# LayerNorm sums taken from additions that are made anyway, a deferred second pass, and two weight slabs from another DMA queue

## The chip, the cores and the metric

The kernel runs on one Trainium2 chip, on all 8 cores (two dies of four), each core with one row of the batch (2048 tokens of 1024). The metric is the device time of the slowest core in microseconds. Some executions fall into a slow state, in which one die is granted a lower clock (0.82 to 0.98 instead of 0.996) and takes up to 18% longer; all comparisons below are between fast executions.

## The reference, cut to what matters

```python
x = layer_norm(ALPHA * x + mix, ln1_w, ln1_b)          # mix: gated convolution and retention, projected
ff = square(relu(x @ w_ff1)) @ w_ff2
ple = sigmoid(x @ w_ple_gate) * (p @ w_ple_proj)
x = layer_norm(ALPHA * x + ff + ple, ln2_w, ln2_b)

def layer_norm(x, w, b):
    mu = mean(x); var = mean(square(x - mu))
    return (x - mu) * rsqrt(var + 1e-5) * w + b
```

A core thus has two LayerNorms over 16 blocks of 128 tokens. The first runs beside retention (blocks 0 to 7) and beside the first feed-forward matmuls (blocks 8 to 15). The second runs in two halves, of which the last ends the kernel. In that last half the second feed-forward matmul is done in seven products (M1 to M7) that VectorE adds into the float32 accumulator `xacc`.

## The kernel before

Helpers record every operation, so all matmuls are "L195" in the profile (transposes on TensorE L199), all `tensor_tensor` L202, all `scalar_tensor_tensor` L213, all activations L226, all DMAs L239. An operation waits for exactly the resources that it names. `bg` is a queue of generators; every `bg.step()` records the next piece of one of them, so the places of `yield` set where LayerNorm stands among the other VectorE work.

```python
# first LayerNorm, blocks 0 to 7 (fine: blocks 0 to 3)
for hf in range(2):
    bn_stats(half hf)                                  # VectorE
    if fine: yield
bn_aggr; rstd = var + eps                              # VectorE
if fine: yield
rstd = pow(rstd, -0.5)                                 # GpSimd
yield
buf = (buf - mean) * w                                 # VectorE, first pass
yield
buf = buf * rstd + b                                   # VectorE, second pass
yield

# statistics of the other blocks: two ScalarE passes over the block, each with an accumulator
def row_stats(b, v, r):
    for k, (fn, sc) in enumerate(((AF.Copy, 1.0 / D), (AF.Square, D ** -0.5))):
        h.act(junk[:], v, fn, [r], ["junk", ("mva", b)], scale=float(sc), accum=lna[:, b, 4 + k:5 + k])

# loads of first-matrix slabs
h.dma("pool", ring[i][:], src, ("ring", i), rd, r)     # all on GpSimd's queue

# last phase, after product (m, p): additions, statistics, and two units later the normalizing
ff2_adds(s_, m, p)
if m == "M4": row_stats(4 + p, ...); due.append((i + 2, 4 + p))
if m == "M5" and p < 3: act_stats(p, 1)
if m == "M7": act_stats(p, 0); due.append((i + 2 - (p == 2), p))
...
# the end: block 3, in two products of 256 columns
ff2_add(3, 0, BANK[1]["M5"] + 3, -1); last_stats(2, 512, 1024)
for q in range(2):
    ...16 matmuls of 256 columns...; xacc -= product; last_stats(q, ...)        # bn_stats
```

Of the kernel before, what the change touches and what calls it, by code (L numbers as in the profile page):

```python
# [17 lines left out]
D = 1024  # L18
# [171 lines left out]
class H:  # L190
# [21 lines left out]
    def stt(self, out, in0, scalar, in1, op0, op1, reads, writes):  # L212
        self.P.op("dve", lambda e: e.scalar_tensor_tensor(out=out, in0=in0, scalar=scalar, in1=in1,  # L213
                                                          op0=op0, op1=op1), reads, writes)
# [91 lines left out]
def build_nc():  # L306
# [59 lines left out]
    lnst = at("lnst", [128, 8, 20], F32, o, [("lnst", i) for i in range(8)]); o += 640  # L366
    lna = at("lna", [128, 8, 8], F32, o, [("lna", i) for i in range(8)]); o += 256
# [77 lines left out]
    xs4 = at("xs4", [128, 4, 512], BF16, o_x1b)  # L445
    hT = at("hT", [128, 32, 1024], BF16, o_sin, [("hT", f, a) for f in range(32) for a in range(2)])
# [5 lines left out]
    with ExitStack() as st:  # L452
# [70 lines left out]
        def load_slab(nm, g, i):  # L523
            r = rname[i]
            if nm in SUMS:
                n = SUMS.index(nm)
                h.dma("sp", ring[i][:], s_w2[n, g], ("ringh", i), [("s_w2", n, g)], r)
                return
            if nm in PRODS[1]:
                nm, g = "ff2", g + {"M2": 0, "M5": 6}[nm]  # L530
            src, rd = wsrc[nm][g], []
            if nm in ("ff1", "gate"):
                k = g + 8 * (nm == "gate")
                src, rd = s_wb[k], [("s_wb", k)]
            h.dma("pool", ring[i][:], src, ("ring", i), rd, r)
# [241 lines left out]
        def gen_ln(buf, rbuf, w_t, b_t, rw, rb, slot, fine=False):  # L777
            st6 = lnst[:, slot, 0:12]
            mv = lnst[:, slot, 12:14]
            rstd = lnst[:, slot, 14:15]  # L780
            rl, rr = ("lnst", slot), ("rstd", slot)
            for hf in range(2):
                P.op("dve", lambda e, hf=hf: e.bn_stats(out=st6[:, hf * 6:(hf + 1) * 6],
                                                        in_=buf[:, hf * 512:(hf + 1) * 512]),
                     [rbuf], [rl])
                if fine:
                    yield
            P.op("dve", lambda e: e.bn_aggr(out=mv, in_=st6), [rl], [rl])
            h.ts("dve", rstd, mv[:, 1:2], LN_EPS, ALU.add, [rl], [rr])
            if fine:  # L790
                yield
            h.tt("pool", rstd, rstd, neghalf[:, 0:1], ALU.pow, [rr, "neghalf"], [rr])
            yield
            h.stt(buf, buf, mv[:, 0:1], w_t[:], ALU.subtract, ALU.mult, [rbuf, rl, rw], [rbuf])
            yield
            h.stt(buf, buf, rstd, b_t[:], ALU.mult, ALU.add, [rbuf, rr, rb], [rbuf])
            yield

        def act_stats(b, hf):

            v = xacc[:, b, hf * 512:(hf + 1) * 512]
            for k, (fn, sc) in enumerate(((AF.Copy, 1.0 / D), (AF.Square, D ** -0.5))):
                h.act(junk[:, 0:512], v, fn, [("xa", b)], ["junk", ("lna", b)], scale=float(sc),
                      accum=lna[:, b, 2 * hf + k:2 * hf + k + 1])

        def row_stats(b, v, r):

            for k, (fn, sc) in enumerate(((AF.Copy, 1.0 / D), (AF.Square, D ** -0.5))):
                h.act(junk[:], v, fn, [r], ["junk", ("mva", b)], scale=float(sc),
                      accum=lna[:, b, 4 + k:5 + k])  # L810

        def act_norm(b, halves=False):

            mv, rstd = lna[:, b, 4:6], lna[:, b, 6:7]
            if halves:
                h.tt("dve", mv, lna[:, b, 0:2], lna[:, b, 2:4], ALU.add, [("lna", b)],
                     [("mva", b)])
            h.stt(rstd, mv[:, 0:1], mv[:, 0:1], mv[:, 1:2], ALU.mult, ALU.subtract,
                  [("mva", b)], [("rsa", b)])
            h.ts("dve", rstd, rstd, -1.0, ALU.mult, [("rsa", b)], [("rsa", b)], s2=LN_EPS,  # L820
                 op1=ALU.add)
            h.tt("pool", rstd, rstd, neghalf[:, 0:1], ALU.pow, [("rsa", b), "neghalf"], [("rsa", b)])

        def norm_pass(k, b, v, r, w_t, rw):


            if k == 0:
                h.stt(v, v, lna[:, b, 4:5], w_t, ALU.subtract, ALU.mult, [r, ("mva", b), rw], [r])
            else:
                h.stt(v, v, lna[:, b, 6:7], w_t, ALU.mult, ALU.add, [r, ("rsa", b), rw], [r])  # L830
# [15 lines left out]
        def mix_part(b, hf, slab, rs, bank):  # L846
# [5 lines left out]
            if b < 8:  # L852
# [3 lines left out]
                  [xr, RP[bank]], [x1r(b)])  # L856
# [3 lines left out]
        def gen_ln1(b):  # L860
            yield from gen_ln(x1v(b), x1r(b), lnt[0], lnt[1], "ln1w", "ln1b", b % 8, b < 4)
# [17 lines left out]
        def gen_norm1(b):  # L879


            act_norm(b - 8)
            yield
            for k in range(2):
                norm_pass(k, b - 8, x1v(b), x1r(b), lnt[k][:], ("ln1w", "ln1b")[k])
                yield
# [99 lines left out]
        for b in range(8, 16):  # L986
# [9 lines left out]
            if 9 <= b < 15:  # L996
                row_stats(b - 9, x1v(b - 1), x1r(b - 1))
# [210 lines left out]
        def phase_ff1_first():  # L1208
# [13 lines left out]
            for n, (g, a) in enumerate(order):  # L1222
# [8 lines left out]
                for f in range(4):  # L1231
# [6 lines left out]
                    if n < 2 and f == 1:  # L1238
                        row_stats(6 + n, x1v(14 + n), x1r(14 + n))
# [165 lines left out]
        def ff2_add(b, hf, bank, sign):  # L1405
            v = xacc[:, b, hf * 512:(hf + 1) * 512]
            h.tt("dve", v, v, ps[bank][:], ALU.add if sign > 0 else ALU.subtract,
                 [RP[bank], ("xa", b)], [("xa", b)])
# [14 lines left out]
        def ff2_adds(s_, m, p):  # L1423
            for (a, hf), sign in PRODS[s_][m][1]:
                ff2_add(4 * a + p, hf, BANK[s_][m] + p, sign)
# [4 lines left out]
        def phase_ff2_first():  # L1430
# [47 lines left out]
            for m in PRODS[s_]:  # L1478
                for i, (j, p) in enumerate(PJ if m in ("M4", "M7") else JP):
# [3 lines left out]
                    if j == 1:  # L1483
                        ff2_adds(s_, m, p)
                        if m in ("M4", "M7"):
                            b = p + 4 * (m == "M4")
                            row_stats(b, xacc[:, b, :], ("xa", b))
# [5 lines left out]
        def phase_ff2_last():  # L1493
# [8 lines left out]
            due = []  # L1502
            for i, (m, p, j) in enumerate(order):
                while due and due[0][0] <= i:
                    bg.add(gen_last(due.pop(0)[1]))
# [8 lines left out]
                if (m, p) == ("M7", 2):  # L1514
                    if j == 0:
                        ff2_add(2, 0, BANK[1]["M5"] + 2, -1)
                    ff2_product(s_, m, j, p, *slabs[m, j], bank=6)
                    if j == 1:
                        ff2_add(2, 0, 6, -1)
                else:  # L1520
                    ff2_product(s_, m, j, p, *slabs[m, j])
                if j == 1:
                    if (m, p) != ("M7", 2):
                        ff2_adds(s_, m, p)
                    if m == "M2":
                        prefetch(30 + 2 * (p == 3))
                    if m == "M4":
                        row_stats(4 + p, xacc[:, 4 + p, :], ("xa", 4 + p))
                        due.append((i + 2, 4 + p))
                    if m == "M5" and p < 3:  # L1530
                        act_stats(p, 1)
                    if m == "M7":
                        act_stats(p, 0)
                        due.append((i + 2 - (p == 2), p))
                bg.step(2 + ((m, p, j) == ("M5", 3, 0)))

            ff2_add(3, 0, BANK[1]["M5"] + 3, -1)
            last_stats(2, 512, 1024)
            for q in range(2):
                qs = slice(q * 256, (q + 1) * 256)  # L1540
                for c in range(16):
                    lt, rl = left(s_, "M7", c, 3)
                    slab, rs = slabs["M7", c // 8]
                    h.mm(ps[7 - 2 * q][:, 0:256], lt, slab[:, c % 8, qs], c == 0, c == 15, rl + rs,
                         [RP[7 - 2 * q]])
                v = xacc[:, 3, qs]
                h.tt("dve", v, v, ps[7 - 2 * q][:, 0:256], ALU.subtract, [RP[7 - 2 * q], ("xa", 3)],
                     [("xa", 3)])
                last_stats(q, q * 256, (q + 1) * 256)
                if q == 0:  # L1550
                    bg.step()
# [6 lines left out]
        st18 = lnst[:, 6:8, :].rearrange("p a b -> p (a b)")[:, 0:18]  # L1558

        def last_stats(k, c0, c1):  # L1560

            P.op("dve", lambda e: e.bn_stats(out=st18[:, k * 6:(k + 1) * 6], in_=xacc[:, 3, c0:c1]),
                 [("xa", 3)], [("lnst", 6), ("lnst", 7)])

        def gen_last(b):

            mv, rstd = lna[:, b, 4:6], lna[:, b, 6:7]
            buf, rb = xacc[:, b, :], ("xa", b)
            if b != 3:
                act_norm(b, b < 4)  # L1570
            else:
                P.op("dve", lambda e: e.bn_aggr(out=mv, in_=st18), [("lnst", 6), ("lnst", 7)],
                     [("mva", b)])
                h.ts("dve", rstd, mv[:, 1:2], LN_EPS, ALU.add, [("mva", b)], [("rsa", b)])
                h.tt("pool", rstd, rstd, neghalf[:, 0:1], ALU.pow, [("rsa", b), "neghalf"],
                     [("rsa", b)])
            yield
            n = 2 if b in (2, 3) else 1
            w_ = D // n
            parts = [(buf[:, k * w_:(k + 1) * w_], slice(k * w_, (k + 1) * w_), (rb, "part", k))  # L1580
                     for k in range(n)]
            for v, cols, r in parts:
                h.stt(v, v, mv[:, 0:1], lnt[2][:, cols], ALU.subtract, ALU.mult,
                      [rb, ("mva", b), "ln2w"], [r])
            yield
            row = (8 + b) * 128
            for k, (v, cols, r) in enumerate(parts):
# [102 lines left out]
```

## Time and profile before

| what | before |
|---|---|
| time, median of 4 runs | 786.84 us (786.61 to 787.08) |
| span of the slowest core in the profile | 785.1 us (core 4) |
| TensorE busy | 749.4 us |
| TensorE waits for the first loads | 13.8 us |
| TensorE waits in the middle | about 10 us |
| from the last matmul's end to the end | 11.67 us |

TensorE is the bound, so only places where it stands still can give time back. The timeline of the kernel before, core 4, near 225 us (start, duration, engine, line, operation, output<-input; in brackets the idle time before, and who ended it):

```profile
224.91 1.27 POOL L202 TENSOR_TENSOR qr<-ra,ra 128x512 bf16<-128x512 f32 x1 [3.05 <-DVE ra L202]
225.29 1.98 DVE L213 SCALAR_TENSOR_TENSOR xacc<-xacc,lnst,ln1b 128x1024 f32<-128x1024 f32 x1
```

The second normalizing pass stands beside GpSimd's rotary sum and takes 1.98 us, where the first pass, alone, takes 1.27. The same view at the end:

```profile
769.76 3.66 PE L195 MATMUL ps<-ring,ring 128*128 128x256 bf16 x32
...
770.76 0.16 DVE L202 TENSOR_TENSOR lna<-lna 128x2 f32<-128x2 f32 x1 [1.73 <-ACT junk L226]
...
777.64 0.42 DVE L202 TENSOR_TENSOR xacc<-xacc,ps 128x256 f32<-128x256 f32 x1 [0.17 <-DVE lnst L1562]
```

VectorE waits 1.73 us for ScalarE's statistics of block 2, and adds the last product at 777.64, while the last matmul ended at 769.76 + 3.66 = 773.42. Call this 4.22 us the *lateness* of the last addition, and the 7.45 us from there to the end of the span the *last chain*. The two sum to the tail of 11.67 us.

### The profile page before, as it was taken

The numbers are of one execution on the slowest core, as the hardware profiler recorded it, in microseconds if no ns is written. First come the engines' busy times: TensorE is split into PE (matmuls) and PEld (weight loads), VectorE is DVE, ScalarE is ACT, GpSimd is POOL, SyncE is SP. The second block draws the span as 40 slices with busy tenths as digits, with TensorE's granted clock in tenths as the row PEclk, the third lists the DMA queues.
The fourth block names the chain that finished last, engine by engine and source line by source line (L and its number), as shares of the span: only waits on it lengthen the run. The fifth ranks groups of instructions, "written<-read, shape, count | busy, mean of one in ns | idle before, by whom it ended". The sixth has DMA issues, their size and how long they took to land.

```text
span 785.1 us, 12424 instructions; the slowest of 8 cores (780.9 to 785.1 us)
## 1 busy us (share of the span) xinstructions
PE 749.4 (95%) x3880; PEld 354.2 (45%) x3880; DVE 538.3 (69%) x743; ACT 343.1 (44%) x688; POOL 211.6 (27%) x242
## 2 busy tenths in 40 slices
PE   3999999999999999998999999999999999999994
PEld 1444445555555445443444444454444444444442
DVE  4565964557975596977756987744666769766666
ACT  2222216554556379585672200067777662100341
POOL 9100025755356401132450000000354450000111
PEclk9999999999999999999999999999999999999997
DMA  9998188981889860788539878477369676376232
GB/s 121 165 172 196 28 110 109 144 150 54 115 122 117 225 202 34 302 262 287 162 134 157 173 233 187 143 221 229 108 208 298 219 240 215 114 180 134 85 141 98
DMA packets 30384, 129.45 MB, mean 165 GB/s; under 512 B 3744, under 2 KB 5920, under 8 KB 23584
## 3 DMA queue, kind: packets, MB, share of 16 engines
q0 software_dynamic: 10160, 50.86, 38.9%
q1 hardware_dynamic: 19296, 76.23, 28.4%
q10 hardware_dynamic: 864, 1.57, 0.6%
q8 instruction: 32, 0.52, 0.3%
q14 instruction: 32, 0.26, 0.1%
HBM read 131.27 MB, written 45.61 MB: 225 GB/s over the span
## 4 chain that ended last, share of the span: by engine, by line
PE 83%; DVE 6%; issue 3%; DMA 3%; POOL 2%; ACT 2%; DVEq 0%; ACTq 0%; POOLq 0%
PE ps L195 81%; DMA xT<-xT 3%; PE ps L199 2%; DVE xacc L202 1%; DVE ring L202 1%; DVE xacc L213 1%; ACT junk L226 1%; POOL lna L202 1%; ACT tR L226 1%; DVE ycat L202 1%; POOL wc L239 1%; DVE ps L202 1%; DVE eb L202 1%; POOL xT L239 1%; DVE ra L202 0%
## 5 line engine op out<-in xcount | busy, mean ns | idle before, releaser
L195 PE MATMUL ps<-ring,ycat 128*128 128x512 bf16 x1088 | 244.0, 379 | 0.3 <-DVE ra L202 0.2
L195 PE MATMUL ps<-ycat,ring 128*128 128x512 bf16 x832 | 184.9, 379 | 4.3 <-DVE ring L202 1.8
L195 PEld LDWEIGHTS ps<-ring,ycat 128*128 128x128 bf16 x1088 | 105.6, 98 | 125.5 <-issue 1.7
L195 PEld LDWEIGHTS ps<-ycat,ring 128*128 128x128 bf16 x832 | 80.7, 98 | 103.1 <-issue 7.5
L195 PE MATMUL ps<-xT,wc 128*128 128x512 bf16 x384 | 86.1, 386 | 13.8 <-DMA wc<-wc 12.9
L202 POOL TENSOR_TENSOR hT<-tR 128x512 bf16<-128x512 f32 x48 | 57.9, 1210 | 149.4 <-ACT tR L226 149.3
L226 ACT ACTIVATE tR<-ps 128x512 f32<-128x512 f32 x128 | 72.7, 595 | 37.6 <-PE ps L195 35.6
L202 DVE TENSOR_TENSOR xacc<-xacc,ps 128x512 f32<-128x512 f32 (+1 forms) x83 | 54.3, 677 | 49.7 <-PE ps L195 47.9
L226 ACT ACTIVATE junk<-xacc 128x1024 fp8e5<-128x1024 f32 (+1 forms) x36 | 32.9, 914 | 84.6 <-DVE xacc L202 78.5
L195 PEld LDWEIGHTS ps<-xT,wc 128*128 128x128 bf16 x384 | 37.4, 99 | 62.0 <-issue 20.2
L195 PE MATMUL ps<-ring,hT 128*128 128x512 bf16 x256 | 56.9, 379 | 0.0
L226 ACT ACTIVATE yn<-ps,colT 128x128 f32<-128x128 bf16 x64 | 29.3, 458 | 47.0 <-PE ps L199 42.5
L202 POOL TENSOR_TENSOR lna<-lna,neghalf 128x1 f32<-128x1 f32 x24 | 25.6, 1066 | 87.5 <-DVE lna L209 80.7
L226 ACT ACTIVATE hT<-tR 128x512 bf16<-128x512 f32 x72 | 45.4, 630 | 4.9
L226 ACT ACTIVATE ycat<-ps 128x1024 bf16<-128x1024 bf16 x16 | 16.2, 1012 | 69.5 <-PE ps L199 69.5
L202 DVE TENSOR_TENSOR ycat<-hT 128x2048 bf16<-128x2048 bf16 x36 | 44.2, 1244 | 1.6
L239 POOL DMA_DIRECT2D ring<-w_ff x12 | 6.5, 546 | 138.7 <-PE ps L195 104.9
L202 DVE TENSOR_TENSOR ring<-ring,ring 128x2048 bf16<-128x2048 bf16 x32 | 38.9, 1221 | 6.0 <-DMA s_w<-ring 2.5
L226 ACT ACTIVATE sg<-ps 128x512 f32<-128x512 f32 x32 | 19.0, 597 | 48.3 <-DVE tR L202 23.3
L202 DVE TENSOR_TENSOR ps<-ps,eb 128x512 f32<-128x512 f32 x48 | 33.6, 700 | 7.8 <-DVE eb L202 3.7
L195 PEld LDWEIGHTS ps<-ring,hT 128*128 128x128 bf16 x256 | 24.9, 98 | 29.3
L202 DVE TENSOR_TENSOR eb<-eb,ps 128x512 f32<-128x512 f32 x24 | 16.4, 685 | 27.3 <-ACT tR L226 27.0
(117 smaller groups left out, 1008.1 us busy)
## 6 DMA issues: line engine op xcount, KB each, us to landing
ring<-s_wb POOLq DMA_DIRECT2D x12, 1024.0 KB, 10.7
ring<-w_ff POOLq DMA_DIRECT2D x12, 1024.0 KB, 11.4
s_w<-ring SPq DMA_DIRECT2D x20, 512.0 KB, 3.5
s_w<-ring SPq DMA_DIRECT2D x10, 1024.0 KB, 5.6
ring<-s_w SPq DMA_DIRECT2D x20, 512.0 KB, 6.6
ring<-s_w SPq DMA_DIRECT2D x10, 1024.0 KB, 7.3
s_wb<-w_ff POOLq DMA_DIRECT2D x8, 1024.0 KB, 15.3
out<-xacc SPq DMA_DIRECT2D x14, 512.0 KB, 3.7
```

The lines of the kernel that those rows point to most:

```text
L195: self.P.op("pe", lambda e: e.matmul(out, lhsT=lhsT, rhs=rhs, start=start, stop=stop, skip_group_check=skip), reads, writes)
L199: self.P.op("pe", lambda e: e.transpose(out=out, in_=in_, identity=ident), reads, writes)
L202: self.P.op(eng, lambda e: e.tensor_tensor(out=out, in0=in0, in1=in1, op=op), reads, writes)
L213: self.P.op("dve", lambda e: e.scalar_tensor_tensor(out=out, in0=in0, scalar=scalar, in1=in1, op0=op0, op1=op1), reads, writes)
L226: self.P.op("act", lambda e: e.activation(out=out, in_=in_, func=func, **kw), reads, writes)
L239: self.P.dma(eng, lambda e: e.dma_start(out=out, in_=in_, **kw), key, reads, writes)
```

## The change

The intent: get the sum of each row from the addition that writes the row (an accumulator output), so that bn_stats goes from VectorE and one of two passes from ScalarE; let the first pass of a block run while ScalarE still squares, and defer the second behind the next product's additions; load two slabs earlier. The core of the diff, cut:

```diff
-            for hf in range(2):
-                P.op("dve", ... e.bn_stats(...))              # and bn_aggr, + eps, pow
+        def squares(n, i, v, r, out=junk, ro="junk"):
+            h.act(out[:, 0:v.shape[-1]], v, AF.Square, [r], [ro, ("sq", n)],
+                  scale=float(D ** -0.5), accum=lns[:, n, i:i + 1])
+        def mean(n):                                          # (sum0 + sum1) / D, VectorE
+        def root(n, halves=False):                            # m*m - squares, VectorE
+            ...
+            h.ts("pool", var, var, LN_EPS, ALU.add, [r], [r])
+            h.tt("pool", var, var, neghalf[:, 0:1], ALU.pow, [r, "neghalf"], [r])
...
             h.stt(x1v(b)[:, cols], xs, ALPHA, ps[bank][:], ALU.mult, ALU.add,
-                  [xr, RP[bank]], [x1r(b)])
+                  [xr, RP[bank]], [x1r(b), ("sm", b)], accum_out=lns[:, b, hf:hf + 1])
...
         def gen_ln1(b):
-            yield from gen_ln(...)
+            squares(...); yield
+            mean(b); root(b); yield
+            for k in range(2):
+                norm_pass(k, ...); yield
...
+            if nm == "ff1" and g in (2, 6):
+                h.dma("act", ring[i][:], src, ("ringa", i), rd, r)
+                return
             h.dma("pool", ring[i][:], src, ("ring", i), rd, r)
...
+            def finish():
+                while second:
+                    next(second.pop(0))                       # the second pass and its store
...
                         ff2_adds(s_, m, p)
                     if m == "M2":
                         prefetch(30 + 2 * (p == 3))
+                    finish()
                     if m == "M4":
-                        row_stats(4 + p, ...); due.append((i + 2, 4 + p))
+                        squares(4 + p, ...)
+                        second.append(gen_last(4 + p))
+                        next(second[0])                       # first pass and root, now
```

The matmuls and their order are the same in both kernels.

## The prediction

> **What bounds the kernel now.** I read the page's busy shares first, then who makes TensorE wait, then busy time by stretch, then the timeline around each place where TensorE stands still. All lines are of the kernel before, core 4, the slowest: span 785.1 us against a median time of 786.84 us, so I carry differences of the span over to the time. The page's first row:
>
> ```profile
> PE 749.4 (95%) x3880; PEld 354.2 (45%) x3880; DVE 538.3 (69%) x743; ACT 343.1 (44%) x688; POOL 211.6 (27%) x242
> ```
>
> TensorE is busy 749.4 us, and 785.1 - 749.4 = 35.7 us is all that a change which leaves the matmuls alone can win. The order of instructions on TensorE and on SyncE is the same in both programs. The waits view (engine, line, waited for: us, times, longest):
>
> ```profile
> PE ps L195 <- DMA wc<-wc: 12.9, 3, 10.9
> PE ps L195 <- DVE ring L202: 2.1, 2, 1.8
> PE ps L195 <- DVE ps L202: 2.1, 4, 0.8
> PE ps L195 <- ACT tR L226: 1.5, 2, 0.8
> PE ps L199 <- POOL kr L202: 1.1, 1, 1.1
> PE ps L199 <- DVE ob L202: 1.1, 1, 1.1
> PE ps L199 <- DVE xacc L202: 0.9, 1, 0.9
> PE ps L195 <- DMA xT<-xT: 0.9, 2, 0.7
> ```
>
> The first and last rows, 13.8 us, are the loads at the start, which the change does not touch. The busy-by-stretch view shows no matmul after 774 us: from the last matmul's end at 773.4 to 785.1 is a tail of 11.7 us. That leaves about 10.2 us in the middle: 2.5 at 200 to 270 us (retention with the first LayerNorm), 3.7 at 340 to 380, 1.0 at 496 to 513, 1.4 at 540 to 556, 0.7 at 636 to 642, 0.2 near 756, the rest crumbs. Two places need their timelines. The first (start, duration, engine; in brackets the idle time before and who ended it):
>
> ```profile
> 338.69 1.11 POOL L239 DMA_DIRECT2D ring<-s_wb  x2
> ...
> 350.74 1.23 DVE L202 TENSOR_TENSOR ring<-ring 128x2048 bf16<-128x2048 bf16 x1 [4.34 <-DMA ring<-s_wb]
> ...
> 354.54 1.22 DVE L202 TENSOR_TENSOR ring<-ring,ring 128x2048 bf16<-128x2048 bf16 x1
> ...
> 355.90 7.93 PE L195 MATMUL ps<-ycat,ring 128*128 128x512 bf16 x36 [1.80 <-DVE ring L202]
> ```
>
> VectorE waits 4.34 us for two weight slabs whose loads GpSimd issued at 338.69, and TensorE then waits 1.80 us for the weight sum. In the full timeline GpSimd issues them only after a store of x1 (336.19) and a power (337.33) ahead of them in its queue. The second place is the tail:
>
> ```profile
> 774.07 1.47 DVE L202 TENSOR_TENSOR xacc<-xacc,ps 128x512 f32<-128x512 f32 x2
> ...
> 775.65 0.69 DVE L1562 BATCH_NORM_STATS2 lnst<-xacc 128x6 f32<-128x512 f32 x1
> 776.51 0.42 DVE L202 TENSOR_TENSOR xacc<-xacc,ps 128x256 f32<-128x256 f32 x1 [0.17 <-DVE lnst L1562]
> ...
> 778.69 0.24 DVE L1572 BATCH_NORM_AGGREGATE lna<-lnst 128x2 f32<-128x18 f32 x1
> ...
> 779.34 0.92 POOL L202 TENSOR_TENSOR lna<-lna,neghalf 128x1 f32<-128x1 f32 x1 [6.77 <-DVE lna L206]
> 780.79 1.41 DVE L213 SCALAR_TENSOR_TENSOR xacc<-xacc,lna,ln2b 128x512 f32<-128x512 f32 x2 [0.28 <-DVE xacc L213]
> ```
>
> Block 3's last three additions start at 774.07, with nearly no gap behind: VectorE is in arrears. The M5 product they need ended at 769.9, but VectorE was still normalizing block 2, for which it had waited 1.73 us on ScalarE's two statistics passes.
>
> **What the Trainium skill says.** "VectorE: DVE Perf Modes", section "Two Vector instructions with no wait between them": an operation that also writes out its accumulator is two instructions, the main one and an accumulator read. No VectorE operation before has one; ScalarE's form shows as 0.18 to 0.22 us of read after each pass. My estimate for VectorE's is 0.1 us. "SBUF — State Buffer", section "Who interferes with whom": a VectorE instruction with two SBUF inputs shuts out a GpSimd instruction that reads SBUF until it is done. The trace agrees: the [128,1] power takes 0.54 us alone and 1.45 beside a 1.28 us normalizing pass. "ScalarE: Activation LUTs", section "What ACT_TABLE_LOAD costs": 186 ns plus 0.833 ns an element with immediate scale; that gives 1.04 us for 1024 and 0.61 for 512, where the trace has 1.06 and 0.63; for the new width of 256 I take 0.40.
>
> **The change part by part.**
> (1) Sums come free with additions that are made anyway: accumulator outputs on the output projection's 32 evictions and on the last addition into each half row. Cost: about 65 reads of 0.1 us, 6 us of VectorE time, nearly all beside matmuls.
> (2) For blocks 0 to 7 of the first LayerNorm, two bn_stats (0.69 each), the aggregate (0.21) and the 0.15 epsilon add go from VectorE; a mean (0.15) and a variance (0.21) come. Saving 1.4 us a block, 11 us in all, against a square pass on ScalarE of 1.06 + 0.18 us each. For 23 of the other 24 row blocks ScalarE loses its Copy pass, the same 1.24 us each (1.6 for the split ones). So both engines are lighter, while GpSimd gets one more small operation a block.
> (3) In retention, 200 to 230 us, the order of VectorE changes: the first normalizing pass (1.28) now stands ahead of the `ob` and `vb` evictions, behind the wait for ScalarE's squares, and the second comes before the rotary products instead of after the masked scores. In before, that second pass ran beside GpSimd's rotary sum and took up to 2.04 us. Going through one 12.5 us round with the row durations, VectorE has 9.5 us of work instead of 11.5. The 1.1 us wait for `kr` goes, but the masked scores come some 1 us later and may cost 0.2 to 0.3 in a round. Net -0.5 us.
> (4) Slabs 2 and 6 are loaded from ScalarE's queue, right after the fourth feed-forward group. That group's matmuls end near 326 (16 groups of 1.73 us and four sets of transposes from 296), 12 us ahead of 338.69; at the same 12 us of transfer the data land near 339, before VectorE wants them at 346.4. The 4.34 us wait goes and so does TensorE's 1.80. The next two slabs, 3 and 7, are still on GpSimd, issued at 355.78 after a store that follows VectorE; they can go at about 352.5, when their slots are free. Of the 0.82 us wait at 373.8, behind a 2.28 us wait for these slabs, about 0.55 goes. Together -2.35 us.
> (5) At 496 to 513 and at 540 to 556 TensorE waits for a VectorE backlog of additions and 1.23 us sums; accumulator reads in it cost +0.1 each: +0.2 us.
> (6) The tail. The first pass of block n now runs while ScalarE squares, and the second is postponed behind the next product's additions, so VectorE waits for nothing. Going by the matmuls' ends: block 2's first pass ends by 768.8, its variance by 769.3, block 3's M5 addition (product done at 769.7) by 770.5, block 2's second pass by 771.9, the two additions ready by then at 773.0. So VectorE is free when the last product ends at 773.2 (0.2 earlier: the wait near 756 goes as well). Then: addition and read to 773.85; 256 squares 0.40 + 0.19 on ScalarE to 774.6; square sum and mean to 775.0; first half pass to 775.7; variance, two small operations 0.33 apart, to 776.1; second half pass to 776.7, GpSimd shut out till then; epsilon and power to 777.7; two half passes to 779.2. Before, that end was at 782.2. Gain 3.0 us, with the 2.9 us of the last output's DMA the same.
>
> Sum: -0.5 - 2.35 + 0.2 - 3.0 = -5.65 us: 786.84 becomes 781.2 us.
>
> **The rivals.**
> A: the accumulator read costs more than 0.1 us, say 0.25, or holds the next instruction. For it: ScalarE's own read is 0.19. Against: VectorE's [128,1] operations take 0.15 and start every 0.33 even when dependent. It would hit the LayerNorm rounds and the tail (M2 and M4 leave VectorE only some 1 us spare in 6.9): 1 to 2 us back, 782.5 to 783.
> B: a new wait in retention. ScalarE's square pass stands in order before the `qkT` copy, and VectorE waits for it with `ob` behind. ScalarE is free from 204.8 to 207.9 in the round I read, and the squares need 206.6 to 207.9: it fits with no margin. If each of four rounds loses 0.5 us, the time is 783.5.
> C: the early load is hidden or collides: slabs 2 and 6 travel with the weight-sum stores, and TensorE finds its next wait at the sums of 357 to 364, which stand in the same order. Against: the DMA share at 270 to 340 is 0.53, and the engines have room. It would give 783.5, with only the tail won.
> D: waits in the middle all vanish, because VectorE has 11 us less to do: then up to 4 us more, 777. Against: `ob` at 266 and the chains at 364 and 553 are latencies through three engines.
>
> **Range and chances.** Steps (4) and (6) rest on timelines that I could follow one by one, and each could miss by 1.5 us; (3) by 1.0. With the rivals this makes 778.6 to 784.2 us. A gain over 2% needs 771.1, so 15.7 us out of the 21.9 that lie outside the start's loads, where the tail cannot vanish: chance 0.01. A loss of 2% would need a new bound, and no engine but TensorE is over 70%: 0.01.
>
> **What would show each step right or wrong.** (1): a read row of about 0.1 us after each accumulating addition. (3): no wait for `kr` near 228, and waits on `PT` or `qkT` below 0.3 us. (4): the slab loads in ScalarE's queue near 327, no idle VectorE before the sum near 346, no 1.80 us wait. (6): the last addition within 0.2 us of the last matmul's end, and some 8.9 us from that end to the span's end instead of 11.7. I am wrong if the slabs land late, if VectorE is still in arrears at the last product, or if TensorE's waits between 190 and 270 us grow.

## The result, and the profile after

The changed kernel takes 781.22 us (median of 9 runs, 781.02 to 781.37), the kernel before 786.52 us (median of its eight fast runs in the same rounds; over all its 13 runs, one of them slow, 786.76). The ratio is 0.9931 with a 95% interval of 0.9921 to 0.9940. A ratio here is the mean time of one kernel's fast runs over that of the other's of the same rounds, so it is not quite the ratio of the medians quoted. The prediction was 781.2 us. The spans of the cores went from 780.9-785.1 to 776.9-779.2 us. The page's first row, and who makes TensorE wait, for the changed kernel, core 7, its slowest (engine, line, waited for: us, times, longest):

```profile
PE 748.7 (96%) x3880; PEld 354.4 (45%) x3880; DVE 527.8 (68%) x792; ACT 327.3 (42%) x658; POOL 219.7 (28%) x272
```

```profile
PE ps L195 <- DMA wc<-wc: 13.5, 4, 10.2
PE ps L195 <- ACT tR L226: 1.7, 2, 0.9
PE ps L195 <- DVE ps L202: 1.3, 3, 0.6
PE ps L199 <- DVE ob L202: 1.0, 1, 1.0
PE ps L199 <- DVE xacc L213: 1.0, 1, 1.0
...
PE ps L195 <- ACT sg L226: 0.4, 1, 0.4
...
PE ps L195 <- DVE PT L202: 0.2, 1, 0.2
```

VectorE and ScalarE are lighter (538.3 to 527.8, 343.1 to 327.3 us), but that alone is worth nothing. What counts is that the waits for `kr` (1.1) and for the weight sum (1.8; a second one of 0.4 stays, in the lines left out) are gone. One wait is new on every whole core: 0.4 us for the gate `sg`. Another, for `tR` just before it, comes on some cores only (0.3 us on core 7, 0.7 on core 4): there VectorE waits for a late slab of the second matrix at 424 us (3.23 and 3.54 us; on core 1 not at all) and is in arrears afterwards. In the kernel before, core 4 waits 2.13 us for it, and TensorE not. The slab loads, same core:

```profile
328.50 1.28 ACTq L239 DMA_DIRECT2D ring<-s_wb  x2
...
344.91 1.23 DVE L202 TENSOR_TENSOR ring<-ring 128x2048 bf16<-128x2048 bf16 x1
...
350.30 0.54 POOL L239 DMA_DIRECT2D ring<-s_wb  x1
```

ScalarE issues slabs 2 and 6 ten microseconds earlier than GpSimd did, and the sum at 344.91 has no bracket: nobody waited. GpSimd issues slab 3 at 350.30 and slab 7 at 351.74, where core 4 before issued both at 355.78. The end, same core:

```profile
766.31 3.66 PE L195 MATMUL ps<-ring,ring 128*128 128x256 bf16 x32
766.59 0.69 DVE L213 SCALAR_TENSOR_TENSOR xacc<-ps,xacc 128x512 f32<-128x512 f32 x1
767.21 0.08 DVE L213 DVE_READ_ACCUMULATOR xacc<-ps,xacc 128x1 f32 x1
767.66 1.41 DVE L213 SCALAR_TENSOR_TENSOR xacc<-yb,lns,ln2b 128x512 f32<-128x512 f32 x2 [0.38 <-POOL lns L202]
769.00 0.68 DVE L213 SCALAR_TENSOR_TENSOR xacc<-ps,xacc 128x512 f32<-128x512 f32 x1
...
770.73 0.42 DVE L213 SCALAR_TENSOR_TENSOR xacc<-ps,xacc 128x256 f32<-128x256 f32 x1 [0.17 <-DVE lns L202]
...
771.87 0.16 DVE L202 TENSOR_TENSOR lns<-lns 128x1 f32<-128x1 f32 x1 [0.70 <-ACT junk L226]
```

The last matmul ends at 766.31 + 3.66 = 769.97, and its addition starts at 770.73: lateness 0.76 us instead of 4.22. The last chain is 8.47 us instead of 7.45, the tail 9.23 instead of 11.67.

Where the time came from, read from the windows view as TensorE's idle time in each stretch. Two cores of each profile lack some matmul records and show 0.3 to 0.7 us more idle in several stretches, so I use whole cores:

| stretch, us | what runs | before, core 4 | after, core 4 |
|---|---|---|---|
| 60-290 | convolution, retention, projection | 2.53 | 1.36 |
| 335-392 | first matrix in seven products | 3.69 | 1.16 |
| 392-470 | end of it, gate | 0.76 | 1.61 (1.04 on four of six whole cores; core 4 has the `tR` wait) |
| 470-600 | second matrix, next first matrix | 2.35 | 2.38 |
| 690-765 | last phase | 0.20 | 0.00 |
| tail | after the last matmul | 11.68 | 9.21 |

The idle time before 60 us, which is the wait for the first loads, differs between cores and runs (10.3 to 14.9 us in the whole cores of all runs here) whatever the kernel. So stretches can be compared to 0.1 us, but for waits that only some cores show, and spans and times only to about half a microsecond.

A point that the slowest core hides: in the kernel before, only cores 0, 2, 4 and 7 paid for the late slabs in full (2.86 to 3.72 us idle at 335-392), while cores 1, 3 and 5 idled 1.06 to 1.19 us there, although GpSimd issued the loads at 337 to 339 us on all. The data landed later on some cores than on others: from the issue to VectorE's sum it took 10.1 to 10.4 us on cores 1, 3, 5 and 6, and 11.9 to 12.1 on the four that paid. That is one core of each neighbouring pair (0/1, 2/3, 4/5, 6/7), and not by chance: in the 22 fast runs of the kernel before beside the experiments, one core of such a pair is above 782.6 us and the other below in 20 or 21 runs, against 9 to 14 for any other two cores. Which of the two it is changes from run to run. This points to something that the two share; no run tested it. Since the slowest core sets the time, the slab part counts in full.

### The profile page after: what moved, and what is told of

It is laid out like the page before. It is cut to its first block, busy times and chain, and to the rows that moved or that the text cites. A ratio compares the mean times of both kernels' runs of the same rounds, so it can differ in the third digit from the quotient of the medians.

```text
span 779.2 us, 12470 instructions; the slowest of 8 cores (776.9 to 779.2 us)
## 1 busy us (share of the span) xinstructions
PE 748.7 (96%) x3880; PEld 354.4 (45%) x3880; DVE 527.8 (68%) x792; ACT 327.3 (42%) x658; POOL 219.7 (28%) x272
## 4 chain that ended last, share of the span: by engine, by line
PE 80%; DMA 7%; DVE 4%; issue 4%; ACT 2%; POOL 2%; DVEq 0%; ACTq 0%; POOLq 0%
PE ps L195 78%; DMA xT<-xT 3%; DMA ring<-w_ff 2%; PE ps L199 2%; DMA ring<-s_wb 2%; ACT tR L226 1%; DVE ring L202 1%; DVE xacc L213 1%; DVE ycat L202 1%; DVE tR L202 1%; POOL wc L239 1%; POOL xT L239 1%; ACT sg L226 0%; DVE xs L202 0%; POOL hT L202 0%
## 5 line engine op out<-in xcount | busy, mean ns | idle before, releaser
L213 DVE SCALAR_TENSOR_TENSOR xacc<-ps,xacc 128x512 f32<-128x512 f32 (+1 forms) x83 | 54.6, 682 | 50.9 <-PE ps L195 49.0
L226 ACT ACTIVATE junk<-xacc 128x1024 fp8e5<-128x1024 f32 (+2 forms) x25 | 22.1, 885 | 104.0 <-DVE xacc L213 103.6
L206 POOL TENSOR_SCALAR lns<-lns 128x1 f32<-128x1 f32 x32 | 17.3, 541 | 101.4 <-DVE lns L213 77.2
```

Of the source, the lines that this page charges most:

```text
L206: self.P.op(eng, lambda e: e.tensor_scalar(out=out, in0=in0, scalar1=s1, scalar2=None, op0=op0), reads, writes)
L213: self.P.op("dve", lambda e: e.scalar_tensor_tensor(out=out, in0=in0, scalar=scalar, in1=in1, op0=op0, op1=op1, **kw), reads, writes)
L226: self.P.op("act", lambda e: e.activation(out=out, in_=in_, func=func, **kw), reads, writes)
```

## The experiments

Each ran in five rounds beside the kernel before on the same chip. The times are medians of the fast runs; their intervals are about 1.2 us wide on either side, so verdicts below a microsecond rest on the traces.

| run | based on | us | before, same chip | ratio, 95% |
|---|---|---|---|---|
| slab_only | before | 784.45 | 786.09 | 0.9978 (0.9963 to 0.9993) |
| slab_undone | after | 783.36 | 786.09 | 0.9963 (0.9949 to 0.9978) |
| order_only | before | 786.65 | 786.09 | 1.0006 (0.9993 to 1.0020) |
| old_order | after | 781.23 | 786.09 | 0.9937 (0.9922 to 0.9952) |
| no_defer | after | 785.85 | 785.88 | 0.9998 (0.9985 to 1.0011) |
| add_first | after | 780.06 | 785.88 | 0.9924 (0.9910 to 0.9938) |
| tail | add_first | 778.56 | 785.88 | 0.9904 (0.9888 to 0.9920) |
| more_reads | after | 780.91 | 785.88 | 0.9933 (0.9920 to 0.9946) |
| defer_first | after | 783.38 | 786.30 | 0.9966 (0.9953 to 0.9979) |
| act_sums | after | 782.62 | 786.30 | 0.9956 (0.9942 to 0.9970) |
| bn_block3 | add_first | 780.00 | 786.30 | 0.9918 (0.9904 to 0.9932) |
| act_shift | after | 780.05 | 786.30 | 0.9921 (0.9907 to 0.9936) |

All gave correct results.

### The slabs: slab_only and slab_undone

slab_only is the kernel before with these three lines; slab_undone is the changed kernel without them.

```diff
+            if nm == "ff1" and g in (2, 6):
+                h.dma("act", ring[i][:], src, ("ringa", i), rd, r)
+                return
             h.dma("pool", ring[i][:], src, ("ring", i), rd, r)
```

> The kernel before, with nothing changed but that first-matrix slabs 2 and 6 are loaded from ScalarE's queue. Theory (step 4 is a gain of its own): the loads are issued near 327 to 330 us on every core, the 4.3 us wait of VectorE before the weight sum near 350 and TensorE's 1.80 us wait go, and TensorE's idle time between 335 and 392 us falls from 3.2-3.7 us to 1.2-1.5 on cores 0, 2, 4 and 7, while cores 1, 3 and 5, which had only 1.2, keep it. The time falls by 2.0 to 2.5 us, to about 784.5. Rival C (the early load is hidden or collides with the stores): TensorE waits elsewhere before 392 us and the time stays within 0.7 us of 786.8.

> The changed kernel with slabs 2 and 6 back in GpSimd's queue. If the slab gain is independent of the rest: 781.2 + 2.35 = 783.5 us, with a DVE wait for a slab of 4 us on some cores. Rival: with less VectorE work GpSimd reaches the load 1 us or more earlier, so part of the gain would have come without the new queue: 781.5 to 782.5. The 0.38 us wait for the gate (sg) near 435 us stays if the statistics make it and goes if the slab load does.

Measured: alone, the lines take 1.6 us off; taken out of the changed kernel, they cost 783.36 against 0.9931 x 786.09 = 780.7, so 2.7 us. The interval of slab_only excludes no gain, and its trace rules out rival C: on cores 0 and 2 TensorE idles 1.16 and 1.43 us at 335-392 instead of 3.17 and 3.72. In slab_undone five of eight cores pay (3.6 to 4.5 us idle there, three have 1.1 to 1.5), though GpSimd issued the loads earlier, at 335.0 to 337.0 instead of 337.4 to 339.0 (TensorE's own work stands about 1.2 us earlier there too). So the lighter statistics would not have won this by themselves.

The part alone gives less on two cores: 4 and 7 still idle 2.25 and 1.98 us in this stretch, not the expected 1.2 to 1.5. The timeline of slab_only, core 7:

```profile
351.53 1.16 POOL L239 DMA_DIRECT2D ring<-s_wb  x2
...
367.71 1.71 DVE L202 TENSOR_TENSOR ring<-ring 128x2048 bf16<-128x2048 bf16 x1 [2.51 <-DMA ring<-s_wb]
```

The next pair, slabs 3 and 7, is still on GpSimd. Here it is issued at 351.53, VectorE waits 2.51 us for it, and TensorE 0.8 behind VectorE. On core 7 of the changed kernel the two are issued at 350.30 and 351.74, VectorE waits 0.84 us, and TensorE not at all. VectorE's wait differs by core in both kernels (0 to 2.5 us in slab_only, 0 to 1.4 in the changed one, on cores 1, 3, 5 and 7), so I say no more than that some 0.8 us of step 4 on the slow cores did not come from the new queue. GpSimd's earlier issue may be its source, but only the first of the two loads is clearly earlier, and the wait is again longest on one core of each pair, so the cause stays open.

The new 0.4 us wait for `sg` is in neither kernel: 392-470 idles 0.75 us in both (one whole core of slab_undone has 0.94, for `tR`). That fits neither half of the expectation; see act_shift.

### Retention: order_only and old_order

order_only is the kernel before with two yields fewer, so that the passes stand where the change puts them; old_order is the changed kernel with two more, so that they stand where they stood before.

```diff
 order_only:
-                if fine:
+                if fine and hf == 0:
                     yield
             P.op("dve", lambda e: e.bn_aggr(out=mv, in_=st6), [rl], [rl])
             h.ts("dve", rstd, mv[:, 1:2], LN_EPS, ALU.add, [rl], [rr])
-            if fine:
-                yield
 old_order:
             yield
+            if b < 4:
+                yield
             mean(b)
             root(b)
             yield
+            if b < 4:
+                yield
```

> The kernel before, bn_stats kept, with only the order of the first LayerNorm changed: the first pass stands ahead of the ob and vb evictions, the second ahead of the rotary products. Theory (the order takes the wait for kr away, because the second pass no longer runs beside GpSimd's rotary sum): TensorE's 1.1 us wait for kr goes, stage 190-235 falls from 1.3 to about 0.3 us, and the time is 0.8 to 1.2 us shorter, about 785.8. Rival (the lighter VectorE does it): bn_stats, 1.4 us more in the same round, now all stands ahead of ob and vb, so TensorE waits for ob or PT instead by 0.5 us or more, and the time is 786.5 to 788.

> The changed kernel with the first LayerNorm's passes back in their old places (first pass behind the vb eviction, second behind the masked scores). Order theory: the second pass runs again beside GpSimd's rotary sum and takes some 1.9 us, the kr wait of about 1 us returns, time 782.2. Work theory: VectorE has 1.4 us less a round, so the wait stays under 0.3 us and the time within 0.3 of 781.2.

The waits view of core 3 from 60 to 235 us, first order_only, then old_order:

```profile
PE ps L195 <- DVE PT L202: 1.6, 4, 0.7
```

```profile
PE ps L199 <- POOL kr L202: 0.6, 1, 0.6
```

With the kernel before (`kr` 1.1, `ra` 0.2) and the changed one (`PT` 0.2) this makes a square. TensorE's idle time on core 3, same stretch:

| | old order | new order |
|---|---|---|
| bn_stats | 1.33 (before) | 1.63 (order_only) |
| sums from the evictions | 0.56 (old_order) | 0.27 (after) |

The order alone loses 0.3 us: with bn_stats all standing ahead of the `ob` and `vb` evictions, the masked scores come late, four times. The lighter work alone gains 0.77, and after it the order gains another 0.3. So neither theory holds by itself: the work carries the gain, and the order changes its sign with it. The pass in old_order again takes 1.98 us beside GpSimd, and `kr` is waited for again, but for half as long.

### The end: no_defer, defer_first, act_sums

no_defer calls `finish()` directly after the first pass, for all blocks; defer_first does it for blocks 0 to 2 alone; act_sums keeps the deferral but has ScalarE make the sums of the last phase in a Copy pass.

```diff
 no_defer (both places) and defer_first (the second only):
                         second.append(gen_last(4 + p))
                         next(second[0])
+                        finish()
 ...
                         second.append(gen_last(p))
                         next(second[0])
+                        finish()
 act_sums:
-            kw = dict(accum_out=lns[:, n, i:i + 1]) if last else {}
+            last_ = last and (s_ == 0 or b == 3)
+            kw = dict(accum_out=lns[:, n, i:i + 1]) if last_ else {}
 ...
+                        copies_(p, 0, xacc[:, p, 0:512], ("xh", p, 0, 0))   # h.act(..., AF.Copy, accum=...)
                         squares(p, 3, xacc[:, p, 0:512], ("xh", p, 0, 0))
```

> The changed kernel with the last phase's second normalizing pass right behind the first, not postponed behind the next product's additions. Theory (the postponement is what frees VectorE at the end): VectorE waits for ScalarE's squares and GpSimd's root before every second pass, block 3's M5 additions come some 1 us later, the last addition starts 0.7 to 1.5 us after the last matmul instead of 0.76, plus 0 to 1 us of TensorE waits between 690 and 765: time 781.9 to 783. Rival (the free sums do it alone, because ScalarE is one pass shorter): within 0.3 us of 781.2.

> The changed kernel with the second pass postponed for blocks 4 to 7 but not for blocks 0 to 2. It splits what the run without any postponement mixed: there a third output store came ahead of two slab loads in SyncE's queue (loads issued at 741.45 instead of 737.21, TensorE waiting 2.8 us for them on the slowest core), and VectorE was 3.10 us late at the last product. Theory: the stores of blocks 4 to 7 alone decide about the loads, so here no wait for the loads between 690 and 765 us, while the last addition still starts some 3.1 us after the last matmul and the tail is 11.8 us: time 781.2 + 2.6 = 783.8. Rival (the arrears come from blocks 4 to 7, whose passes are twice as long): the last addition within 1.5 us, time under 782.5.

> The changed kernel with the postponement kept, but the sums of blocks 0 to 2 and 4 to 7 of the last phase made by a ScalarE Copy pass ahead of the square pass, as in the kernel before, instead of by the additions' accumulators. If the postponement alone carries the gain at the end: VectorE's first pass waits about 0.8 us (Copy of 512 columns 0.63 + read 0.19) for the mean, but the waits fit into its spare time except at block 2, time 781.2 to 781.7. If the free sums are needed too: VectorE is 0.8 to 1.2 us later at the last product, the last addition starts some 1.7 us after the last matmul, time 782.0 to 782.5.

no_defer missed what was expected (781.9 to 783 us, the last addition 0.7 to 1.5 us late): it takes 785.85 us, so the deferral is worth nearly the whole change. Half of that was unforeseen. The waits view of no_defer, core 7, from 560 us, and SyncE's queue in the timelines, first of the changed kernel, then of no_defer:

```profile
PE ps L195 <- DMA ring<-s_w: 2.8, 2, 1.6
```

```profile
727.96 7.24 SPq L239 DMA_DIRECT2D out<-xacc  x2
737.21 2.06 SPq L239 DMA_DIRECT2D ring<-s_w  x2
```

```profile
727.05 14.24 SPq L239 DMA_DIRECT2D out<-xacc  x3
741.45 1.15 SPq L239 DMA_DIRECT2D ring<-s_w  x2
```

SyncE issues in order. Without the deferral a third output store stands ahead of two slab loads in its queue. The store waits for VectorE's pass, so the loads go 4.2 us later and TensorE waits 2.8 us (0.4 to 2.8 by core). The deferral puts the store behind `prefetch`, and nobody had asked for that. The kernel before had the loads first too, by its two units of delay. defer_first confirms it: with blocks 4 to 7 deferred there is no wait for a load from 690 to 765 us on any whole core, while the rest of the loss stays, at 783.38 us where 783.8 was expected.

The rest is VectorE's arrears. The end of the kernel, from all runs (lateness of the last addition behind the last matmul, last chain from there to the end, us; the cores of a run agree within 0.2, but for two of add_first below with a last chain of 8.9):

| kernel | free sums | deferred | lateness | last chain | tail |
|---|---|---|---|---|---|
| before | no | two units | 4.22 | 7.45 | 11.67 |
| no_defer | yes | no | 3.10 | 8.71 | 11.81 |
| defer_first | yes | not blocks 0-2 | 3.18 | 8.57 | 11.75 |
| act_sums | no | yes | 2.38 | 8.50 | 10.87 |
| after | yes | yes | 0.76 | 8.47 | 9.23 |

Neither half does it: without the deferral nothing of the tail is won, without the free sums 0.8 us. Without the deferral VectorE waits 1.20 us for GpSimd's root before every second pass; of no_defer, core 7:

```profile
771.52 1.42 DVE L213 SCALAR_TENSOR_TENSOR xacc<-yb,lns,ln2b 128x512 f32<-128x512 f32 x2 [1.20 <-POOL lns L202]
```

With the deferral but without the free sums it waits for ScalarE before the first pass; of act_sums, core 7:

```profile
765.59 0.21 DVE L209 TENSOR_SCALAR lns<-lns 128x1 f32<-128x1 f32 x1 [0.92 <-ACT junk L226]
```

Its last addition is 2.38 us late, not the 1.7 expected. With both, the lateness is 3.46 us less than before. Not all of that is theirs: block 3's bn_stats also left the way of the last addition, which bn_block3 below puts at 0.9 us, and in return the last chain has become 1.0 us longer. The tail's 2.44 us is what counts.

### The last chain: add_first, tail and bn_block3

add_first moves block 3's additions ahead of (half of) block 2's second pass. tail also rebuilds block 3's variance so that only the last 256 squares are waited for, adds epsilon in the same VectorE operation and leaves GpSimd one operation. bn_block3 is add_first with bn_stats for block 3.

```diff
 add_first:
-                    finish()
+                    if (m, p) != ("M5", 3):
+                        finish()
 ...
             ff2_add(1, 3, 0, ps[bank][:], RP[bank], -1, False)
+            next(second[0])                      # first half of block 2's second pass
             for q in range(2):                   # the other half follows the first addition
 tail, on top:
+                    h.tt("dve", lns[:, 3, 6:7], lns[:, 3, 2:3], lns[:, 3, 3:4], ALU.add, ...)    # squares so far
+                h.stt(var, m, m, var, ALU.mult, ALU.subtract, ...)                   # m*m - squares so far
 ...
-                    inverse_root(3)
+                    h.stt(var, lns[:, 3, 5:6], LN_EPS, var, ALU.add, ALU.subtract, ...)
+                    h.tt("pool", var, var, neghalf[:, 0:1], ALU.pow, ...)
```

> The changed kernel with block 3's second M5 addition and its first 256-column addition moved ahead of (half of) block 2's second pass. Theory (VectorE is 0.5 to 0.6 us in arrears at the last product because that addition stands behind a pass that waits for GpSimd's root): the last 256-column addition starts about 0.2 us after the last matmul's end instead of 0.76 after, and the time falls by 0.5 us, to 780.7. Rival (the arrears cost nothing, as ScalarE's squares or the output transfers end last): no change, 781.2.

> As the run before, and block 3's end shortened as well: the first half sums of squares are subtracted from the squared mean before the last squares arrive, epsilon is added in the same VectorE operation as the last squares, so that GpSimd has one small operation left, and that one lies beside the second half pass. Worked out from the changed kernel's rows: the mean at once behind the last addition's read (no 0.70 us wait for ScalarE), one GpSimd operation of 0.57 us and its 0.7 of start taken off: 0.8 to 1.0 us less than the run before, 779.8 in all. If the power cannot be hidden behind the half pass, 780.3.

> The run with block 3's additions first, and block 3's statistics by bn_stats again instead of sums and squares. From the traces: from the start of the last addition to the end of the span the changed kernel takes 8.47 us, the kernel before with bn_stats 7.45. Theory (the new statistics lengthen the last chain by 1.0 us, through ScalarE's square pass, three small VectorE operations in a row and a second GpSimd operation): this chain is 7.4 to 7.5 us here, while VectorE has 1.0 us of bn_stats more ahead of it and is 0.9 to 1.0 us late at the last product, so tail 8.4 and time 780.0, a draw. Rival (the length is in the passes and the store): chain 8.4, tail 9.4, time 781.0.

| kernel | lateness | last chain | tail |
|---|---|---|---|
| after | 0.76 | 8.47 | 9.23 |
| add_first | 0.10 | 8.42 | 8.52 |
| bn_block3 | 1.00 | 7.32 | 8.32 |
| tail | 0.10 | 7.32 | 7.42 |

All three came as expected or a little better. add_first shows that the lateness was real time: 0.66 us less, and the tail is 0.7 us shorter. bn_block3 shows that the new statistics, not the passes or the store, lengthened the last chain: with bn_stats it is 7.32 us again, and the bn_stats that VectorE now does before the last addition (0.69 and 0.43 us) come back as 0.9 us of lateness, a draw on the fast runs' medians. tail has both ends. Its core 1:

```profile
769.55 0.42 DVE L213 SCALAR_TENSOR_TENSOR xacc<-ps,xacc 128x256 f32<-128x256 f32 x1 [0.25 <-PE ps L195]
...
771.21 0.15 DVE L213 SCALAR_TENSOR_TENSOR lns<-lns 128x1 f32<-128x1 f32 x1
771.40 0.75 DVE L213 SCALAR_TENSOR_TENSOR yb<-xacc,lns,ln2w 128x512 f32<-128x512 f32 x1
771.51 1.05 POOL L202 TENSOR_TENSOR lns<-lns,neghalf 128x1 f32<-128x1 f32 x1 [4.47 <-DVE lns L213]
772.73 1.42 DVE L213 SCALAR_TENSOR_TENSOR xacc<-yb,lns,ln2b 128x512 f32<-128x512 f32 x2 [0.58 <-POOL lns L202]
```

VectorE now waits for TensorE at the last product. The power takes 1.05 us beside VectorE's half pass (0.57 alone) and is not quite hidden; 0.58 us of wait remain. At 778.56 us (three fast runs) tail beats both kernels: its whole interval, 0.9888 to 0.9920, lies below the changed kernel's.

### The cost of a read: more_reads

```diff
-            kw = dict(accum_out=lns[:, n, i:i + 1]) if last else {}
+            spare = st4[:, fk[0] % 2, fk[0] // 2 % 12:fk[0] // 2 % 12 + 1]
+            kw = dict(accum_out=lns[:, n, i:i + 1] if last else spare)
```

> The changed kernel with 48 accumulator reads more (every addition of the two second-matrix phases writes one out, to a spare column). Theory: 0.08 us of VectorE each, 3.9 us in all, nearly all beside matmuls: TensorE's idle time at 470-600 us grows by 0.2 to 0.4 us and the time by 0.2 to 0.4, to 781.5. Rival A (a read holds the next instruction, 0.25 us or more each in a backlog): TensorE's idle time there grows by 1 us or more, time 782.2 or above.

Measured: 780.91 us, ratio 0.9933, the same as the changed kernel's 0.9931. The trace shows 83 reads behind additions into `xacc` instead of 33, at 83 ns each, so 50 more (I had counted 48) and 4.1 us more of VectorE. On core 1 TensorE's idle time at 470-690 goes from 3.09 to 3.18 us. Even the expected 0.2 to 0.4 us was too much: rival A is out where this run puts reads, and the reads elsewhere are as short (82 to 83 ns).

### The new wait for the gate: act_shift

```diff
         rotary_setup()
+        for k in range(2):
+            h.act(sqj[:, k:k + 1], posf[:, k:k + 1], AF.Copy, ["posf"], [("sqk", k)])
```

> The changed kernel with two one-element copies more on ScalarE, at its very start, and nothing else. It is about the wait for the gate (sg) near 435 us, 0.38 us, which every kernel with the changed kernel's ScalarE instructions shows on every core and neither the slab load alone nor the statistics alone does. If it hangs on the place of the instruction in ScalarE's stream, it goes: stage 392-470 idles 0.76 us instead of 1.04, time 780.9. If it comes from data, buffers or transfers, it stays at 1.04 and the time at 781.2.

ScalarE's timeline on core 1, first the changed kernel, then act_shift:

```profile
434.46 0.60 ACT L226 ACTIVATE sg<-ps 128x512 f32<-128x512 f32 x1 [1.84 <-PE ps L195]
```

```profile
434.20 0.60 ACT L226 ACTIVATE sg<-ps 128x512 f32<-128x512 f32 x1 [1.45 <-PE ps L195]
```

The wait is gone on all six whole cores: 392-470 idles 0.69 us instead of at least 1.04, and three other stretches (335-392, 470-600, 600-690) 0.07 us less each on most of them. Two tiny copies 400 us earlier, on an engine that is idle more than half of the time, touch no data, buffer or transfer of the gate. So the wait hangs on where the instruction stands in ScalarE's stream (or on another effect of two instructions more that I can't name), and not on the sums or the slabs. By what mechanism stays open: the profile shows nothing there that ScalarE waits for beyond the product. The gain is small and the time's interval (0.9907 to 0.9936) doesn't prove it; the stretch does.

## Why the prediction was right

The total was right to 0.1 us, which is in part luck: the errors of the steps cancelled, and the kernel before was itself 0.3 us faster beside the changed one than the 786.84 that the prediction started from. As a change, -5.65 us was predicted and -5.4 measured (0.69% of 786.5). Step by step, against core 4 or the tables above:

| step | predicted | measured | verdict |
|---|---|---|---|
| (3) retention | -0.5 | -1.2 | direction right, mis-sized |
| (4) slabs | -2.35 | -2.5 | right |
| (5) reads in backlogs | +0.2 | +0.03 | too dear |
| (6) tail | -3.0 | -2.6 | right mechanism, mis-sized |
| not foreseen: `sg` | 0 | +0.3 (core 4 has 0.6 more, for `tR`) | missed |

The measured steps sum to -6.0 us (without the `tR` wait), against -5.9 in the slowest cores' spans and -5.3 in the medians. The remainder lies within what the first loads vary.

**(1)** The estimate of 0.1 us for VectorE's accumulator read was good: 0.083 us. The Trainium skill, "VectorE: DVE Perf Modes", section "Two Vector instructions with no wait between them", gives the second instruction but no duration; the trace shows both. more_reads showed that reads beside matmuls cost TensorE nearly nothing, which makes (5) too dear.

**(3)** The text named two causes, the lighter VectorE (2 us a round) and the second pass leaving GpSimd's company, and subtracted 0.2 to 0.3 us a round for late masked scores. The square of four kernels shows the lighter work as the cause (-0.77), and the order as worth +0.3 or -0.3 depending on it. The term that was mis-sized is "may cost 0.2 to 0.3 in a round": it measured 0.2 in all. `kr` gave its 1.1, a 0.2 us wait for `ra` went unforeseen, and 0.1 came at 235 to 290. The foreseen cost did exist, in order_only: 1.6 us in four waits.

**(4)** The issue near 327 (326.9 to 328.5), the sum without a wait and the missing 1.80 stood as written; the next pair was issued at 348.7 to 351.7, a little ahead of the 352.5 written. Its last 0.55 us measured 0.7, but slab_only, whose next pair is as early as written, did not win it on cores 4 and 7, so the reason given for it is not shown. What the text didn't say is that only some of the cores had the 1.80 us wait at all.

**(6)** "VectorE waits for nothing" failed in one place. Block 2's second pass waited 0.38 us for GpSimd, and block 3's second M5 addition stood behind it, so the last addition came 0.76 us after the last matmul instead of within 0.2. The tail was 9.23 us instead of 8.9; with the 0.2 us wait at 756, which did go, the step gave 2.6. add_first took exactly this term away. The reason given, first pass beside the squares and second pass behind the additions, was right: defer_first and act_sums show that each without the other leaves the tail at 11.75 and 10.87 us. Two things were missed. The deferral also decides the order of stores and loads in SyncE's queue (2.8 us in no_defer). And leaving bn_stats makes the last chain 1.0 us longer, which the prediction's own figures held (a tail of 8.9 us with an addition that is at most 0.2 us late) without saying that bn_stats would have been shorter there.

**Rivals.** A fell with more_reads, C with slab_only. B's wait did not come: `PT` costs 0.2 us in all. D did not happen either: `ob`, ScalarE's `tR` and `xacc` are waited for as before.

## What to carry to other kernels

Free statistics and a deferred pass were worth little singly and 2.4 us together, so test the parts of a change in both directions, alone and taken out, before crediting one of them. A pass moved on one engine also moves its store in an in-order DMA queue; look at what load stands behind it. Where throughput counts, take sums from operations that are made anyway; in the very last chain count the operations in a row instead. There bn_stats was 1.0 us shorter than the sums as first arranged, and the sums, rearranged in the run tail, were as short (7.32 us) without making the last addition late.

## What the Trainium skill lacked or had wrong

- The duration of VectorE's accumulator read is missing on "VectorE: DVE Perf Modes", section "Two Vector instructions with no wait between them", which has the instruction: 83 ns here, less than half of ScalarE's 0.19 us.
- "SBUF — State Buffer", section "Who interferes with whom", has the lock between VectorE and GpSimd, and the runs agree; no size is given for small operations. A [128,1] epsilon add on GpSimd took 0.22 us alone and up to 1.11 us beside a 1.28 us pass, a power 0.57 and 1.05 to 1.45 us. Nor is one for the other way round: the 1.27 us pass took 1.98 us beside a GpSimd sum.
- I found no page with a figure for a ScalarE instruction starting later or earlier when others are put far ahead of it: 434.46 against 434.20 us, 0.35 us of TensorE. The nearest is "Runtime: NRT & Kernel Launch", section "Instruction fetch mechanics"; no run shows whether that is the cause.
- I found no figure for how much the landing of the same load differs between the two cores of a neighbouring pair; it belongs to "HBM Reference". From issue to use it took 10.1 to 10.4 us on one core and 11.9 to 12.1 on the other, and TensorE idled 1.1 us on some cores and 3.7 on others after loads issued within 2 us of each other.
